# One encoder layer with grouped experts: entry order, first expert pair, and the order of the last factors

## The chip, the cores and the metric

The kernel runs on one core of a Trainium2 chip. The metric is the device time of one execution in microseconds. The kernel before took 590.38 us as the median of three runs (590.33 to 591.84).

## The reference

Input x is (1, 512, 1024) in float32. One layer is computed, cut here to its order:

```python
h = layer_norm(x, ln_emb_g, ln_emb_b)
proj = h @ w_in                     # 1024 x 1824: qa, ka, va, cq, ckv, kr
out_a = windowed_gqa_sink(...)      # 8 heads of 64, keys within 128 positions, a sink per head
out_b = mla_attention(...)          # 8 heads, low-rank q (768) and kv (256), all keys
h = layer_norm(2**0.25 * h + concat(rms_norm(out_a), rms_norm(out_b)) @ w_out, ...)
# experts: the best of 4 groups, in it the best 2 of 8; 32 experts of 1024 -> 256 -> 1024
for e in range(32):
    y += combine[:, e:e+1] * ((silu(h @ w_gate[e]) * (h @ w_up[e])) @ w_down[e])
h = layer_norm(2**0.25 * h + y, ln_ffn_g, ln_ffn_b)
```

## The kernel before, in words

The 512 tokens are four tiles of 128 rows (t = 0 to 3); 1024 features are eight blocks of 128. Most products of the first part are made of three: each operand is split into a rounded high half (a copy on ScalarE) and a low half (a subtraction, mostly on VectorE), `split` at line 208, and `mm3` at 213 to 215 multiplies high by high, high by low and low by high.

**Entry.** SP issues x, then gain and bias of the first norm spread over all partitions (line 144), the constants, and the first chunk of `w_in` in four quarters (line 161). `layer_norm` (line 199) makes z[t] of x with two VectorE operations per half (lines 203 and 204); TensorE turns z into eight blocks (line 257), and their halves are `hth` and `htl`. The weight halves of the first chunk are split with their low part on GpSimd (line 209). Products of tile 0 with the first chunk are ordered by what arrives (line 385); all others run through `mm3`. z itself stays in memory as the residual.

**Middle.** Three more chunks of `w_in`, the low-rank key and query products (units of 4 heads and a tile; `heads` turns them, line 468), attention B, attention A, and the output projections, which add into z. Here the order on the engines is a planner's: it simulates the program and issues what is ready first, by order of the text, with a few orders laid down by `issue_after`.

**From the last attention tile to the end** the order on all engines is the written one (`manual_schedule`). The last two tiles (a = 2, b = 3) are normed, routed (`route`: ten small VectorE steps that end in the tile's expert mask), counted (`count`: products with a triangle, `place`: the row's place in its expert) and selected (`select`: a 0/1 matrix of 64 places per expert). The rows of the first expert pair are gathered by products (`gather`, line 1131); later pairs are fetched by an indirect DMA on GpSimd from the normed rows in HBM (`fetch`, line 1056), into which `keep` (line 847) writes them from ScalarE's queue.

**Experts.** They run in 16 pairs, 64 rows of each expert. A pair p takes eight blocks of gate and up products for both experts (`gates`, line 1265; 512 columns), `gated` (line 1269 on), the down products (`down`, line 1285), the weighted add into the rows (line 1298) and an indirect DMA that writes them to HBM (`scatter`, line 1291). Between hid and its transpose and after it, `meanwhile` does other work. Weights are 3 MB for each expert, in a ring of six slots, so three pairs are in memory or on their way. Slots 0 and 1 hold the gate weights of blocks 0 to 3 as two tiles of 512 KB and those of blocks 4 to 7 as one of 1 MB (`gu_tiles`); the other slots have two of 1 MB. A load into a slot waits until the products that read the old tile are done, and SP issues loads in order. `load_next(p)` asks for pair p + 3.

In pair 0 two blocks of gates go first, then the place products of pairs 0 to 3 (line 1394), the row numbers (lines 1027 to 1035) and four fetches, and the weights of the routing (lines 927 to 935); the other six blocks follow.

**End.** The last pair's rows go by products with the transposed selection (`pz_part`, lines 1332 and 1334) onto the rows read back from HBM; `total`, `square`, `factor` (a power on GpSimd, line 183), `gain_first` (line 1548) and `scale_bias` (line 1553) norm them, and SP writes them out.

## Time and profile before

| | |
|---|---|
| median of three runs | 590.38 us (590.33 to 591.84) |
| the profiled execution | 591.72 us, its span 590.0 us |
| TensorE busy | 532.0 us (90%) |
| VectorE busy | 319.1 us (54%) |
| ScalarE busy | 221.9 us (38%) |
| GpSimd busy | 97.3 us (16%) |
| DMA moved | 141.76 MB, mean 240 GB/s |

The span is the time from the first to the last instruction; the rest of an execution lies around it. Busy shares are means over stages that have different limits, so the rows below are taken by stretch. PE is TensorE, PEld its weight loads, DVE VectorE, ACT ScalarE, POOL GpSimd, SP the engine that issues most DMAs; L1265 is line 1265 of the kernel before. The granted clock is a share of full speed. What stands in brackets behind an instruction is the idle time ahead of it on its engine and what ended it.

### The profile page before, as it was taken

The page shows a single profiled execution, that of the slowest core. Times are in us where ns is not written, and L with a number is a line of the kernel's source. Part 1 is how long each engine was busy: PE and PEld are TensorE (multiplying, and loading weights), DVE is VectorE, ACT ScalarE, POOL GpSimd, SP SyncE. Part 2 cuts the span into 40 slices and gives each one's busy share as a digit, 9 for nine tenths or more (in the row PEclk, how much of TensorE's full clock was granted, in tenths as well). Part 3 has the DMA queues.
Part 4 walks back from the last instruction along what each step waited for, and adds up shares of the span by engine and source line. Part 5 has one row for each costly group of instructions (what it writes and reads, how often), then busy time and mean ns, then how long its engine had stood idle before and what let it go on. Part 6 is the DMA issues. An engine that isn't in the chain of part 4 may idle for free. (4 is left out here: it accounts for less than half of the span.)

```text
span 590.0 us, 8025 instructions
## 1 busy us (share of the span) xinstructions
PE 532.0 (90%) x2772; PEld 334.5 (57%) x2773; DVE 319.1 (54%) x870; ACT 221.9 (38%) x481; POOL 97.3 (16%) x139
## 2 busy tenths in 40 slices
PE   2899999999898999999998899999997699879883
PEld 1688898799765777677777444343432233314241
DVE  5955473765687757947768734434434222102266
ACT  2356442454587738856731312211111111102123
POOL 2701121311100000213200201122111101100031
PEclk9999999999898999999999989999999989979988
DMA  8982400121210005991266899999999999999673
GB/s 288 294 275 72 142 3 1 58 82 41 84 46 27 1 1 207 292 355 50 65 261 248 293 389 398 420 417 414 414 415 395 422 418 386 415 420 417 256 284 142
DMA packets 46267, 141.76 MB, mean 240 GB/s; under 512 B 12379, under 2 KB 19419, under 8 KB 37008
## 3 DMA queue, kind: packets, MB, share of 16 engines
q1 hardware_dynamic: 40608, 131.06, 58.8%
q0 software_dynamic: 4464, 8.06, 3.7%
q10 hardware_dynamic: 1152, 2.10, 0.9%
q8 instruction: 23, 0.38, 0.3%
q14 instruction: 20, 0.16, 0.1%
HBM read 133.14 MB, written 16.25 MB: 253 GB/s over the span
## 5 line engine op out<-in xcount | busy, mean ns | idle before, releaser
L1265 PE MATMUL p_gu<-w_gu,xT 128*64 128x512 f32 x512 | 125.4, 614 | 15.2 <-DMA w_gu<-in_w_gu 14.3
L1265 PEld LDWEIGHTS p_gu<-w_gu,xT 128*64 128x64 f32 x512 | 39.0, 141 | 96.8 <-issue 72.1
L1269 ACT ACTIVATE hid<-p_gu 128x256 f32<-128x256 f32 x16 | 6.1, 383 | 176.6 <-PE p_gu L1265 164.7
L1270 DVE TENSOR_TENSOR hid<-hid,p_gu 128x256 f32<-128x256 f32 x16 | 6.7, 421 | 113.8 <-ACT hid L1269 113.7
L1285 PE MATMUL p_y<-w_dn,hidT 128*64 128x512 f32 x256 | 59.8, 610 | 1.0 <-issue 0.6
L1298 DVE SCALAR_TENSOR_TENSOR xg<-p_y,wsl,xg 128x512 f32<-128x512 f32 x30 | 22.5, 751 | 28.3 <-PE p_y L1285 27.6
L604 PE MATMUL ptr<-cst,pr 128*128 128x128 f32 x208 | 34.0, 283 | 1.9 <-ACT pr L562 1.4
L1285 PEld LDWEIGHTS p_y<-w_dn,hidT 128*64 128x64 f32 x256 | 17.5, 140 | 31.3 <-issue 29.2
L1056 POOL DMA_INDIRECT xg<-norm_rows,tok x16 | 16.5, 1029 | 102.5 <-PE p_y L1285 16.6
L1291 POOL DMA_INDIRECT moe_rows<-xg,idx x15 | 15.5, 1036 | 98.1 <-DVE xg L1298 72.6
L604 PEld LDWEIGHTS ptr<-cst,pr 128*128 128x128 f32 x208 | 25.3, 146 | 9.4 <-ACT pr L562 2.8
L577 ACT ACTIVATE pr<-pmm,bnm 128x512 f32<-128x512 f32 x32 | 22.0, 687 | 12.0 <-DVE bnm L574 10.7
L574 DVE TENSOR_REDUCE bnm<-pmm 128x1 f32<-128x512 f32 x32 | 21.9, 687 | 7.1 <-PE pmm L215 6.8
L215 PE MATMUL pmm<-wh,htl 128*128 128x512 f32 (+1 forms) x64 | 23.9, 374 | 0.0
L213 PE MATMUL pmm<-wh,hth 128*128 128x512 f32 (+1 forms) x64 | 23.8, 372 | 0.0
L214 PE MATMUL pmm<-wl,hth 128*128 128x512 f32 (+1 forms) x64 | 23.5, 368 | 0.0
L562 ACT ACTIVATE pr<-pr,rc 128x512 f32<-128x512 f32 (+2 forms) x32 | 20.6, 645 | 4.1 <-DVE rc L560 3.8
L590 DVE CUSTOM_DVE_ANT_0 sm<-pmm,mask,nsink 128x256 f32<-128x256 f32 (+1 forms) x32 | 17.4, 544 | 7.7 <-PE pmm L587 6.5
L215 PE MATMUL pwo<-wh,htl 128*128 128x512 f32 (+1 forms) x56 | 20.7, 370 | 0.0
L214 PE MATMUL pwo<-wl,hth 128*128 128x512 f32 (+1 forms) x56 | 20.5, 367 | 0.0
L213 PE MATMUL pwo<-wh,hth 128*128 128x512 f32 (+1 forms) x56 | 20.5, 367 | 0.0
L1254 ACT ACTIVATE xg<-xg,of 128x1024 f32<-128x1024 f32 x15 | 17.2, 1148 | 8.5 <-PE p_x L1250 7.8
(348 smaller groups left out, 1166.8 us busy)
## 6 DMA issues: line engine op xcount, KB each, us to landing
w_gu<-in_w_gu SPq DMA_DIRECT2D x52, 1024.0 KB, 16.3
w_dn<-in_w_dn SPq DMA_DIRECT2D x20, 1024.0 KB, 18.5
w_gu<-in_w_gu SPq DMA_DIRECT2D x24, 512.0 KB, 16.6
w_dn<-in_w_dn SPq DMA_DIRECT2D x24, 512.0 KB, 14.4
wf<-in_w_in SPq DMA_DIRECT2D x12, 512.0 KB, 6.5
moe_rows<-zr SPq DMA_DIRECT2D x8, 512.0 KB, 7.5
rows<-moe_rows SPq DMA_DIRECT2D x8, 512.0 KB, 8.3
wf<-in_w_q_b SPq DMA_DIRECT2D x12, 192.0 KB, 2.3
```

The costliest lines, as they stand in the source:

```text
L213: PE.matmul(ps, ah, bh, start=first, stop=False)
L214: PE.matmul(ps, ah, bl, start=False, stop=False)
L215: PE.matmul(ps, al, bh, start=False, stop=last)
L562: SC.mul(pr[:, :n], pr[:, :n], rc)
L574: V.tensor_reduce(nm, sp, AX.X, ALU.max, negate=True)
L577: exps_.append(SC.activation(pr[:, :S], sp, AF.Exp, bias=nm, accum_out=den).ins)
L590: V.tensor_tensor_reduce(sm[:, :nk], sp[:, :nk], mask[:, mo:mo + nk], 1.0, nsink[:, h:h + 1], ALU.add, ALU.min, nm)
L604: PE.transpose(pt[:, k * P:(k + 1) * P], pr[:, k * P:(k + 1) * P], ident)
L1254: SC.mul(pl["xg"], pl["xg"], pl["of"])
L1265: PE.matmul(pg[64 * i:64 * i + 64], xT[:, j, 64 * i:64 * i + 64], ws[i][0][j], start=(j == 0), stop=(j == 7))
L1285: r = PE.matmul(py[64 * i:64 * i + 64, :], hT[:, j, 64 * i:64 * i + 64], ws[i][1][n][:, j], start=(j == 0), stop=(j == 1))
L1298: V.scalar_tensor_tensor(y, py, pl["wsl"], y, ALU.mult, ALU.add)
```

## The change

**Entry.** Gain and bias come in as columns (`ge_T`, one number per feature and partition) and are applied after the transposes: ScalarE scales and shifts x by the row's statistics into z, TensorE turns it, and `gain_x` applies gain and bias to 128x128 blocks on VectorE or ScalarE. The order for tiles 0 and 1 on VectorE, ScalarE, TensorE and GpSimd is written out; the low weight halves are made on VectorE. z then lacks gain and bias; they are loaded later and put on in the query units, half a tile behind each unit's `heads`.

**Routing.** Tile a's second gain and bias stand earlier, `route(a)` is stopped after five steps and resumed later, counts and places move, tile a and b are gathered from the second half, `rows_of` stands ahead of the copies of xT, and the rest of the routing goes behind the first place products.

**First pair.** The gate blocks run in the order 4 to 7, 0 to 3; behind the first of them come the place products of pairs 0 and 1 alone, their rows and the fetches 1 and 0, then the routing's end, then the other seven blocks. The places of pairs 2 and 3 come behind hid. After both halves of the down products, `between` makes the place products with the weights for four pairs, then pair 1's columns, then the residual, and only then the weighted adds. In slots 0 and 1 the second half of the gate weights is now in two tiles of 512 KB and the first in one of 1 MB; pair 3 loads the second half first, for both experts in turns.

**End.** `factor` stands one or more steps earlier.

```diff
+        geT = cp.tile([P, 2, NK], F32, name="geT")
+        SC.dma_start(out=cst, in_=A["cst"][:, :C_KEEP])
+        SC.dma_start(out=geT, in_=A["ge_T"])
         load_x(0)
-        lg, lb = [lp.tile([P, D], F32, name=nm) for nm in ("lng", "lnb")]
-        for n in range(2):
-            for dst, nm in ((lg, "ln_emb_g"), (lb, "ln_emb_b")):
-                SY.dma_start(out=dst[:, 512 * n:512 * n + 512], in_=A[nm][512 * n:512 * n + 512].partition_broadcast(P))
-        SY.dma_start(out=cst, in_=A["cst"][:, :C_KEEP])
...
-                split(wf[:, :, :n], wh[:, :, :n], wl[:, :, :n], PO if nch[0] == 0 else V)
+                if nch[0]:
+                    split(wf[:, :, :n], wh[:, :, :n], wl[:, :, :n])
+                else:
+                    wfs.append(wf)
...
-            layer_norm(xs[t], z[t], lg, lb)
+        chunks.append(chunk_load([(768, 512)]))
+        for t in range(2, NT):
+            load_x(t)
...
+        def scaled_x(t, kk):
+
+            rs, nb = nrm[t]
+            sl = slice(512 * kk, 512 * kk + 512)
+            SC.activation(z[t][:, sl], xs[t][:, sl], AF.Identity, scale=rs, bias=nb)
+
+        def turn_x(t, kk):
+            pt = ptr()
+            for k in range(4):
+                PE.transpose(pt[:, k * P:(k + 1) * P], z[t][:, (4 * kk + k) * P:(4 * kk + k + 1) * P], ident)
+            tur[t, kk] = pt, lp.tile([P, 4, P], F32, name="hf", bufs=2)
...
+        def gain_x(t, kk, ks, eng):
+            pt, hf = tur[t, kk]
+            for k in ks:
+                g_, b_ = [geT[:, i, 4 * kk + k:4 * kk + k + 1] for i in range(2)]
+                if eng is SC:
+                    SC.activation(hf[:, k], pt[:, k * P:(k + 1) * P], AF.Identity, scale=g_, bias=b_)
+                else:
+                    V.tensor_scalar(hf[:, k], pt[:, k * P:(k + 1) * P], g_, b_, ALU.mult, ALU.add)
...
+        def high(t, kk):
+            SC.copy(hth[at(t, kk)], tur[t, kk][1])
+
+        def low(t, kk):
+            V.tensor_tensor(htl[at(t, kk)], tur[t, kk][1], f32v(hth[at(t, kk)]), ALU.subtract)
+
+        def w_high(q):
+            SC.copy(chunks[0][1][q][0], wfs[q])
+
+        def w_low(q):
+            V.tensor_tensor(chunks[0][1][q][1], wfs[q], f32v(chunks[0][1][q][0]), ALU.subtract)
...
+        with tc.manual_schedule(engines={V.engine, SC.engine, PE.engine, PO.engine}):
+            stats_half(0, 0)
+            stats_half(0, 1)
+            stats_end(0)
+            stats_shift(0)
...
+                scaled_x(0, kk)
+                turn_x(0, kk)
+            gain_x(0, 0, range(4), V)
+            w_high(0)
+            stats_half(1, 0)
+            gain_x(0, 1, (1,), SC)
+            high(0, 0)
+            first_mm(0, hth, 0, 0)
+            low(0, 0)
+            first_mm(0, htl, 0, 0)
+            gain_x(0, 1, (3,), SC)
+            gain_x(0, 1, (0, 2), V)
+            w_high(1)
+            first_mm(0, hth, 1, 0)
+            first_mm(0, htl, 1, 0)
+            stats_half(1, 1)
+            stats_end(1)
+            high(0, 1)
+            low(0, 1)
+            stats_shift(1)
+            w_high(2)
+            first_mm(0, hth, 2, 0)
+            first_mm(0, htl, 2, 0)
+            for kk in range(2):
+                scaled_x(1, kk)
+                turn_x(1, kk)
+            w_low(0)
+            w_high(3)
+            first_mm(0, hth, 3, 0)
+            first_mm(0, htl, 3, 0)
+            gain_x(1, 0, range(4), V)
+            high(1, 0)
+            gain_x(1, 1, (0, 2), V)
+            gain_x(1, 1, (1, 3), SC)
+            low(1, 0)
+            high(1, 1)
+            low(1, 1)
+            first_mm(0, hth, 0, 1)
+            for q in range(4):
+                first_mm(1, hth, q, 0)
+                first_mm(1, htl, q, 0)
+            for q in range(1, 4):
+                w_low(q)
+                first_mm(0, hth, q, 1)
+            for q in range(4):
+                first_mm(1, hth, q, 1)
+        for t in range(2, NT):
...
+                if kk:
+                    gain_x(t, kk, range(4), SC)
+                else:
+                    gain_x(t, kk, range(4), V)
+                high(t, kk)
+                low(t, kk)
...
-                heads(qt_, qth, qtl, c, t)
+                with tc.issue_after(heads(qt_, qth, qtl, c, t)):
+
+                    zt = z[t][:, 512 * c:512 * c + 512]
+                    V.tensor_tensor(zt, zt, lgb[0][:, c], ALU.mult)
+                    V.tensor_tensor(zt, zt, lgb[1][:, c], ALU.add)
...
-        def load_turns(e, slots):
-
-            ws = [[], []]
-            for h in range(2):
+        def gu_tiles(slot, i):
+            if i == 1 and slot < 2:
+                return [(f"gu{slot}1{q}", 4 + 2 * q, 2) for q in range(2)]
+            return [(f"gu{slot}{i}", 4 * i, 4)]
+
+        def load_gus(e, slot, eng=SY):
+            return load_gu(e, slot, 0, eng) + load_gu(e, slot, 1, eng)
+
+        def load_turns(e, slots, order):
+
+            ws = [{}, {}]
+            for h in order:
                 for ts in zip(*[gu_tiles(sl, h) for sl in slots]):
                     for i in range(2):
-                        ws[i] += load_blocks(e + i, slots[i], *ts[i])
...
         norm_bias(a, 0)
+        norm_gain(a, 1)
+        norm_bias(a, 1)
         logits(a, 0)
         logits(a, 1)
...
         wout_l(1, p1_)
-        steps(route(a))
-        place(1)
+        ra = route(a)
+        steps(ra, 5)
         turn(b, 0)
-        count(a)
         add_z(1, p1_)
...
         rsqrt(rs, mv[:, 1:2], 1.0, LN_EPS / ALPHA ** 2)
         negmean(b)
         turn(b, 1)
-        place(a)
+        steps(ra)
+        place(1)
         sel0_(1)
-        sel0_(a)
         logits(b, 0)
         logits(b, 1)
         offset(b)
         for i in (1, 0):
             scaled(b, i)
-        norm_gain(a, 1)
         biased(b)
-        norm_bias(a, 1)
         for i in range(2):
             keep(a, i)
         gather(0, range(2))
+        count(a)
         gather(1, range(2))
         steps(route(b))
+        place(a)
+        sel0_(a)
         count(b)
-        gather(a, [0])
         gain(b, 1, V)
+        gather(a, [1])
         place(b)
         sel0_(b)
-        gather(a, [1])
+        gather(a, [0])
+        shift(b, 1, V)
         gain(b, 0, V)
-        shift(b, 1, V)
         shift(b, 0, V)
         gather(b, [1, 0])
         for i in (1, 0):
             keep(b, i)
         xT0 = wk[0].tile([P, NK, P], F32, name="xT", bufs=3)
+        for t in (1, a, b):
+            rows_of(t)
         SC.copy(xT0[:, 4:8], gk[1])
         V.tensor_copy(xT0[:, 0:4], gk[0])
-        for t in (1, a, b):
-            exps(t)
-        silu = wk[0].tile([P, 1], F32, name="silu", bufs=1)
-        V.memset(silu, 0.0)
-
-        SC.activation(silu, silu, AF.Silu)
-        for t in (1, a, b):
-            rows_of(t)
-        sels[1] = [select_tile(2, t) for t in range(NT)]
...
-        def down(hT, ws, put):
+        def down(hT, ws, put, between=None):
+            pys = []
             for n in range(2):
                 py = ps.tile([P, 512], F32, name="p_y", tag="pwo", bufs=2)
                 for j in range(2):
                     for i in range(2):
                         r = PE.matmul(py[64 * i:64 * i + 64, :], hT[:, j, 64 * i:64 * i + 64],
                                       ws[i][1][n][:, j], start=(j == 0), stop=(j == 1))
-                put(slice(512 * n, 512 * n + 512), py)
+                pys.append(py)
+                if not between:
+                    put(slice(512 * n, 512 * n + 512), py)
+            if between:
+                between()
+                for n in range(2):
+                    put(slice(512 * n, 512 * n + 512), pys[n])
             return r.ins
...
-                gus = load_turns(e, (s0, s1)) if p + 3 == NP - 1 else [load_gus(e, s0), load_gus(e + 1, s1)]
-                ws[p + 3] = [(gu, None) for gu in gus]
+                if p == 0 or p + 3 == NP - 1:
+
+                    ws[p + 3] = [(gu, None) for gu in load_turns(e, (s0, s1), (0, 1) if p else (1, 0))]
+                else:
+                    ws[p + 3] = [(load_gus(e, s0), None), (load_gus(e + 1, s1), None)]
...
-        def run_pair(p, xT, meanwhile):
+        def run_pair(p, xT, meanwhile, between=None):
             pg = new_gates()
             if p == 0:
-                gates(pg, xT, ws[p], 0, 2)
-                pi = psd("places")
-                for t in range(NT):
-                    for u in range(4):
-                        PE.matmul(pi[:, 2 * u:2 * u + 2], (sel0[t], sels[1][t])[u // 2][:, P * (u % 2):P * (u % 2) + P],
-                                  cmb[t][:, 2 * u:2 * u + 2, 0], start=(t == 0 and u == 0), stop=(t == NT - 1 and u == 3))
-                for g in range(2):
-                    for u, pl in enumerate(places_rows(pi[:, 4 * g:4 * g + 4], 2, 2, 1)):
-                        plc[2 * g + u] = pl
-                        fetch(2 * g + u, pl)
-                for t in range(1, NT):
-                    weights(t)
-                gates(pg, xT, ws[p], 2, 8)
+
+                order = 4, 5, 6, 7, 0, 1, 2, 3
+                gates(pg, xT, ws[p], order, 0, 1)
+                first_rows(0, sel0)
+                routing_end()
+                gates(pg, xT, ws[p], order, 1)
             else:
-                gates(pg, xT, ws[p], 0, 8)
+                gates(pg, xT, ws[p])
             load_next(p)
-            r = leave_rows(gated(pg, meanwhile), ws[p], plc[p])
+            r = leave_rows(gated(pg, meanwhile), ws[p], plc[p], between)
             load_next_dn(p)
             return r
...
+        def first_rows(g, sel):
+
+            pi = psd("places")
+            for t in range(NT):
+                for u in range(2):
+                    PE.matmul(pi[:, 2 * u:2 * u + 2], sel[t][:, P * u:P * u + P], cmb[t][:, 4 * g + 2 * u:4 * g + 2 * u + 2, 0],
+                              start=(t == 0 and u == 0), stop=(t == NT - 1 and u == 1))
+            for u, pl in enumerate(places_rows(pi, 2, 2, 1)):
+                plc[2 * g + u] = pl
+            for q in ((1, 0), (2, 3))[g]:
+                fetch(q, plc[q])
+
+        def routing_end():
+
+            sels[1] = [select_tile(2, t) for t in range(NT)]
+            for t in (1, a, b):
+                exps(t)
+            silu = wk[0].tile([P, 1], F32, name="silu", bufs=1)
+            V.memset(silu, 0.0)
+
+            SC.activation(silu, silu, AF.Silu)
+            for t in range(1, NT):
+                weights(t)
...
                 if p == 0:
                     if i == 0:
-                        residual(0)
-                    else:
-                        pi = psd("places")
-                        places_mm(pi, sel0, [weights_of(u) for u in range(2)], range(NT))
-                        places_weights(pi, [plc[0], plc[1]], 6, 3, 1)
+                        first_rows(1, sels[1])
                     return
...
-            last = run_pair(p, xT, meanwhile)
-            if p == 0:
+            def between():
+                for u, sel in ((0, sel0), (2, sels[1])):
+                    pi = psd("places")
+                    places_mm(pi, sel, [weights_of(u + v) for v in range(2)], range(NT))
+                    places_weights(pi, [plc[u], plc[u + 1]], 6, 3, 1)
+
                 for i in range(2):
                     columns(plc[1], i, nx)
-                pi = psd("places")
-                places_mm(pi, sels[1], [weights_of(2 + u) for u in range(2)], range(NT))
-                places_weights(pi, [plc[2], plc[3]], 6, 3, 1)
+                residual(0)
+            last = run_pair(p, xT, meanwhile, None if p else between)
+            if p == 0:
                 group_sel(2)
             elif p == 1:
...
-        y2 = [ring(slots(p)[0], f"gu0{k}", [P, D], F32R, "y2") for k in range(2)]
+        y2 = [ring(slots(p)[0], f"gu1{k}", [P, D], F32R, "y2") for k in range(2)]
...
         gain_first(0)
         total(1)
         square(1)
+        factor(0)
         gain_first(1)
-        factor(0)
+        factor(1)
         scale_bias(0)
         total(2)
         square(2)
-        factor(1)
         scale_bias(1)
         gain_first(2)
+        factor(2)
         total(3)
         square(3)
         gain_first(3)
-        factor(2)
+        factor(3)
         scale_bias(2)
-        factor(3)
         scale_bias(3)
```

## Rows read from the trace of the kernel before

**Rows 1.** Busy time by stretch: length, five engines, granted clock, DMA share, GB/s

```profile
200.00:295.00 95.00, 93.96 (x549) 70.70 (x549) 66.17 (x207) 63.03 (x166) 16.89 (x44) 1.00 0.44 151
...
320.00:330.00 10.00, 8.77 (x69) 6.92 (x68) 8.04 (x34) 3.07 (x11) 0.00 (x0) 1.00 1.01 404
330.00:342.00 12.00, 10.02 (x52) 5.00 (x53) 7.56 (x43) 1.76 (x4) 4.25 (x4) 0.89 0.79 255
...
340.00:342.00 2.00, 2.00 (x7) 0.75 (x8) 0.48 (x3) 0.00 (x0) 0.00 (x0) 0.50 0.88 346
```

**Rows 2.** TensorE's waits, 330 to 570 us: total, times, longest

```profile
PE p_gu L1265 <- DMA w_gu<-in_w_gu: 14.3, 8, 4.1
```

**Rows 3.** The entry: groups by line (minimum, median, maximum ns) and instructions in time

```profile
L209 POOL TENSOR_TENSOR wl<-wf,wh x4: 2380/2652/2847, 12.1 to 20.6; 128x1024 fp32r<-128x1024 f32 x4
...
L204 DVE SCALAR_TENSOR_TENSOR z<-z,ln_rs,lnb x8: 735/742/2844, 7.7 to 29.7; 128x512 f32<-128x512 f32 x8
...
3.67 1.36 DVE L192 BATCH_NORM_STATS2 ln_st<-xt 128x6 f32<-128x512 f32 x2 [2.63 <-DMA xt<-in_x]
...
L323 DVE SCALAR_TENSOR_TENSOR rp<-pwo,rq,ctb x4: 337/344/352, 132.3 to 153.6; 128x128 f32<-128x128 f32 x4
...
L209 DVE TENSOR_TENSOR htl<-ptr,hth x4: 631/670/690, 11.1 to 25.8; 128x512 fp32r<-128x512 f32 x4
...
40.79 1.23 DVE L209 TENSOR_TENSOR wl<-wf,wh 128x1024 fp32r<-128x1024 f32 x1 [0.97 <-ACT wh L208]
...
31.22 0.39 PE L213 MATMUL pwo<-wh,hth 128*128 128x512 f32 x1
```

**Rows 4.** Query stage and first attention: stretches, one operation's price, GpSimd's additions

```profile
130.00:155.00 25.00, 23.26 (x140) 22.18 (x139) 13.56 (x36) 10.76 (x22) 4.70 (x9) 1.00 0.19 61
155.00:175.00 20.00, 19.42 (x109) 13.47 (x108) 16.74 (x39) 16.11 (x37) 0.45 (x1) 0.91 0.12 32
...
322.12 0.68 DVE L1144 TENSOR_TENSOR z<-z,lngb 128x512 f32<-128x512 f32 x1
...
L332 POOL TENSOR_TENSOR qtok<-rp,rp x8: 454/458/1205, 133.1 to 155.7; 128x128 f32<-128x128 f32 x8
```

**Rows 5.** The first expert pair in time: start, duration, engine, line

```profile
326.71 0.69 DVE L1230 COPY xT<-p_g 128x512 f32<-128x512 f32 x1 [1.54 <-PE p_g L1131]
...
327.46 1.94 PE L1265 MATMUL p_gu<-w_gu,xT 128*64 128x512 f32 x8 [0.78 <-DVE gn L914]
...
329.32 1.95 PE L1394 MATMUL psd<-cmb,sel 128*128 128x2 f32 x16
...
331.20 5.37 PE L1265 MATMUL p_gu<-w_gu,xT 128*64 128x512 f32 x24
...
338.07 0.42 DVE L1270 TENSOR_TENSOR hid<-hid,p_gu 128x256 f32<-128x256 f32 x1
...
339.98 5.02 PE L1285 MATMUL p_y<-w_dn,hidT 128*64 128x512 f32 x16
...
346.74 5.80 PE L1265 MATMUL p_gu<-w_gu,xT 128*64 128x512 f32 x26
...
356.38 3.65 PE L1285 MATMUL p_y<-w_dn,hidT 128*64 128x512 f32 x16
```

**Rows 6.** SP's load issues for the fourth pair, merged and alone

```profile
329.42 9.15 SPq L696 DMA_DIRECT2D w_gu<-in_w_gu  x6
...
333.16 0.33 SPq L696 DMA_DIRECT2D w_gu<-in_w_gu  x1
```

**Rows 7.** The last pair's gates and the last two outputs in time

```profile
555.49 3.65 PE L1265 MATMUL p_gu<-w_gu,xT 128*64 128x512 f32 x14 [1.30 <-DMA w_gu<-in_w_gu]
...
583.10 1.42 DVE L1553 SCALAR_TENSOR_TENSOR rows<-rows,st,gb 128x512 f32<-128x512 f32 x2 [0.66 <-POOL st L183]
...
585.25 1.42 DVE L1553 SCALAR_TENSOR_TENSOR rows<-rows,st,gb 128x512 f32<-128x512 f32 x2 [0.66 <-POOL st L183]
```

More of the change, by code (lines that the diff above doesn't have):

```diff
@@ L1298, in put @@
                 V.scalar_tensor_tensor(y, py, pl["wsl"], y, ALU.mult, ALU.add)
-            r = down(hT, ws, put)
+            r = down(hT, ws, put, between)
             scatter(pl)
@@ L1494, in build @@
                     pg = new_gates("pwo")
[L1495 removed]
+                    gates(pg, xT2, w_)
                     leave_rows(gated(pg), w_, pl)
```

121 lines of the change are left out of this document (68 added, 53 removed).

## The prediction, made before the result was known

> **What bounds the kernel now.** I read the stages first (busy time by stretch), then what TensorE waits for, then the queue that issues the loads, then the instructions around the first expert pair and at both ends. The reader is to see three regimes in [rows 1]. Up to about 310 us TensorE is the bound: 93.96 of 95 us busy between 200 and 295, and VectorE and ScalarE have room. From about 320 on the expert weights are: 404 GB/s in the ten microseconds from 320, and after the prefetched pairs are used up TensorE stands 14.3 us in eight waits for gate weights [rows 2]. Between these lies one hole: from 330 to 342 the transfers reach only 255 GB/s. After the last weights a tail of VectorE work ends the run. So an early saving counts as long as TensorE is dense, a saving in the hole counts because the stream never idles afterwards, and a saving in the tail counts in full. All sums are against the profiled execution, 591.72 us (span 590.0 and 1.72 around it). It lies near the top of the three runs, 1.34 above their median of 590.38, so I take the same difference off the median.
>
> **The entry.** Removed: the broadcast loads of gain and bias (four of 256 KB) ahead of the first weights, the two-step layer norm on VectorE, and the low halves of the first weight chunk on GpSimd. There each of four took 2.65 us, and the VectorE steps beside them stretched from 0.74 to 2.84 us [rows 3]. Added: ScalarE scaling of the rows, gain and bias on the transposed blocks (12 of 128x128 on ScalarE, 20 on VectorE), the weight lows on VectorE, and a written order for tiles 0 and 1. What matters is when tile 2's products can begin, since TensorE is dense behind them; before, tile 2's second product is at 31.22. VectorE's work up to there, after the change: six half statistics of 0.68 (4.1), 16 gains, priced by the 128x128 read from PSUM at 0.34 (at its pitch 0.3: 4.8), six low halves of 0.67 (4.0), four weight lows of 1.23 (4.9), three small chains of about 1 (3.0): 20.8 from 3.67 on gives 24.5. The first chain cannot be filled (factor on GpSimd, one scaling, eight transposes of a cold start): about 3 more, 27.5. Tile 2's transposes are behind both times, so the gain is near 31.0 - 27.5 = 3.5; I take **3.0**. From above: if tile 2's statistics slip into VectorE's gaps, 2.4 less work stands ahead, 5.4. From below: if ScalarE, which now carries scalings, casts and gains, sends VectorE waiting another 3 us, 0. The loads of the next chunk are issued earlier than now, as their buffers are freed earlier.
>
> **The residual gain and bias** come back as 16 VectorE operations of 128x512 on z, two behind each of the eight query units. Price 0.68 each, as the same operation on the same shape takes later [rows 4]: 10.9. Where they go VectorE has 25 - 13.56 = 11.4 us free while TensorE is busy 23.26 of 25 [rows 4], so most is covered by TensorE's products; the last two units' four operations (2.7) lie beside the first attention units, where VectorE is the busier engine (16.74 of 20). I take **+1.0**; ends 0 and 10.9. GpSimd's rope additions stand next to these operations: eight of 0.458 median, one of 1.205.
> The Trainium skill, page "SBUF — State Buffer", section "SBUF: two separate sides", says that VectorE operations with two SBUF inputs and GpSimd operations that read SBUF lock each other out of a shared port for a whole instruction. The trace bears this out at the entry (the 2.84 above). By that rule the removed GpSimd work is worth more, but here it speaks against the change: each new z operation may hold a rope addition, on which a query unit's transposes wait. The time that this would give is in the last rival.
>
> **Routing.** Moving tile a's second gain and bias forward fills VectorE time in which it waits for logits; stopping route(a) after five steps lets z of the last tile go first, about 1.3 us earlier, and the gathers close some 0.6 earlier. This does not move the restart of the weight stream, which hangs on the last projection product. The three row writes move into VectorE's wait of 1.54 ahead of its half of xT [rows 5]; without that cover they would cost 1.2. The gates begin with the half that ScalarE copies, so they need not wait for VectorE's 0.69: start about 326.4 instead of 327.46.
>
> **The ring's first release.** Now: of six gate loads for pair 3 the first is issued at 329.42, the second at 333.16, and the last is out 9.15 after the first began, since the second and third wait for later blocks and hold the other expert's loads behind them in SP's queue [rows 6]. After: one block (5.37 / 6 = 0.9), eight place products instead of 16 (half of 1.95), a second block: 329.2, and there **two** loads of 512 KB go, two more at 331.0, the two of 1 MB at 334.6. So 4.2 MB are asked for by 334.6 instead of 338.6. The hole is worth 12 x (404 - 255) / 404 = 4.4 us by bytes and 12 x 0.21 = 2.5 by DMA share [rows 1]. What is late next is pair 1's release. Pair 0 afterwards: select, exponents and weights keep VectorE until about 336, hid then instead of 338.07; the second rows (1.2 on VectorE, on the path between hid and its transpose) put the down products at 338.1 instead of 339.98; they take 3.65 as in pair 2 instead of 5.02; place products 2.0, columns 1.1, copy 0.6: gates of pair 1 at 345.5 instead of 346.74 [rows 5]. The stream is fed until about 349.6 and pair 1's first release comes near 349.0, so almost all of the gain holds: **3.3**, ends 1.0 and 4.4. The fetches change place: 1 before 0, and 2 and 3 behind hid; pair 2's columns need theirs only some 16 us later. The first pair's residual and scatter go about 2.5 later on ScalarE and GpSimd; the next user of that buffer is a fetch some 14 us behind.
>
> **The tail.** The last pair's final loads are now two blocks instead of four. TensorE waited 1.30 for the last one and then worked 3.65 [rows 7]; after, half of that follows: 1.8, taken as **1.6**, with 0 as the lower end if down weights or the rows read back arrive later. Putting factor(t) ahead of other VectorE work takes away the two waits of 0.66 for GpSimd's factor and the small step in front of each: **1.4** (0.7 to 1.4).
>
> **The sum:** -3.0 + 1.0 - 3.3 - 1.6 - 1.4 = -8.3. That is 583.4 for the profiled execution and 590.38 - 8.3 = **582.1** at the median.
>
> **Rivals.**
> A, the hole only moves: TensorE idles around the first hid as now (two idle stretches of about 1.2), its granted clock falls again to 0.50, the lower of the two levels, as in 340 to 342 [rows 1], the down products take 5.02, pair 1's release is late and the stream runs dry there. Ring term 1.0: 584.4. For it: the same idle did it before. Against: the idle stretches are shorter, with products between them.
> [...]
> B, the entry gives nothing and the z operations cost 3: 590.38 + 3 - 3.3 - 3.0 = 587.1. For it: four engines in a written order, each waiting for another. Against: 3.5 us of loads taken out of the way.
> C, it does not do what it says: the stream is not what ends, since the last pairs are paced by TensorE. Ring and last load nil: 590.38 - 3.0 + 1.0 - 1.4 = 587.0. Against: the 14.3 us of waits, of which the last is in the last pair. B and C together: 592.0.
> D, slower: the z operations lie on the path. All 16 uncovered and each of eight rope additions held as long as the longest (0.75) cost 10.9 + 6.0 = 16.9 against 9.3 of gains: 598.0. It decides from 55% of that price. For it: VectorE is 84% busy right behind, and the planner may spread the operations into attention. Against: 11.4 us free where they are issued.
>
> **How the numbers follow.** Forecast 0.60, A 0.13, B 0.06, C 0.04, B with C 0.05, D 0.12. A measurement here tells about 0.3%, 1.8 us, from no change. Faster: 0.60 + 0.13 + 0.06 + 0.04 = 0.83; same 0.05; slower 0.12. Low end: entry 5.4, ring 4.4, z 0, tail 3.2 give 577.4, rounded to 577.0; the high end takes in A, B and C: 588.5.
>
> **What would show it.** Tile 2's first product by 28; no stretch below 350 GB/s between 330 and 342; pair 1's gates near 345.5 minus the entry's gain; TensorE's last wait for gate weights followed by half as many products; no VectorE wait for the factor in the last two tiles. Wrong if attention starts no earlier than now, or if the hole reappears behind pair 1's gates.

## The result, and the profile after

Median before 593.58 us (590.33 to 595.50, 20 runs), after 590.32 (588.05 to 594.10, 20 runs): ratio 0.995, 95% interval 0.9934 to 0.9967. The change saves 3.0 us (2.0 to 3.9), where 8.3 were forecast. The forecast was also set off a median of three runs, 590.38; over twenty the kernel before stands 3.2 higher, so the absolute time missed by both. In what follows a ratio is turned into us with 593.3, and what stands in brackets behind a ratio or a saving is its 95% interval.

The runs of one kernel scatter over 4 to 8 us, and the mean granted clock of TensorE goes with it: over the 20 runs of the changed kernel -3.0 us per 0.01 of it (correlation -0.71). One profile therefore can't stand for a kernel; steps are compared below over the profiles of all kernels that share the code of the step. The profile of the changed kernel itself is of 592.95 us, and has a fall of the clock to 0.50 (309.7 to 316.6, in the routing) that ten of the thirteen profiles with this routing lack.

The stretches of the changed kernel that answer to [rows 1] (columns as there):

```profile
320.00:330.00 10.00, 9.77 (x83) 8.54 (x82) 9.01 (x34) 2.10 (x3) 0.12 (x1) 1.00 1.00 399
330.00:342.00 12.00, 10.01 (x52) 4.59 (x52) 8.44 (x50) 3.10 (x12) 3.40 (x4) 0.94 1.02 412
342.00:346.00 4.00, 4.00 (x16) 1.08 (x12) 0.00 (x0) 0.00 (x0) 0.85 (x1) 0.77 0.99 392
352.00:356.00 4.00, 4.00 (x22) 1.29 (x18) 2.19 (x6) 0.00 (x0) 1.10 (x1) 1.00 0.71 216
```

The hole of 330 to 342 is gone (255 GB/s then, 412 now), and a smaller one stands at 352 to 356 (216 GB/s, where the kernel before has 376), as rival A said. TensorE's waits over the whole run, against [rows 2]:

```profile
PE p_gu L1383 <- DMA w_gu<-in_w_gu: 11.3, 4, 4.3
PE pz L1457 <- DMA rows<-moe_rows: 2.6, 1, 2.6
```

Four of the eight waits for gate weights are gone, 3.0 us of 14.3, and a new one is there: for rows read back in the tail. The first pair, TensorE, VectorE and SP in time, against [rows 5, 6]:

```profile
329.02 1.08 PE L1383 MATMUL p_gu<-w_gu,xT 128*64 128x512 f32 x4
...
338.47 0.42 DVE L1388 TENSOR_TENSOR hid<-hid,p_gu 128x256 f32<-128x256 f32 x1
...
338.94 0.44 PE L1392 MATMUL p_t<-cst,hid 128*128 128x128 f32 x2 [0.72 <-DVE hid L1388]
...
340.17 0.43 DVE L1394 COPY hidT<-p_t 128x256 f32<-128x256 f32 x1
...
340.65 5.24 PE L1404 MATMUL p_y<-w_dn,hidT 128*64 128x512 f32 x16 [1.27 <-DVE hidT L1394]
...
349.38 0.65 PE L1383 MATMUL p_gu<-w_gu,xT 128*64 128x512 f32 x2 [0.24 <-ACT xT L1368]
...
332.11 5.95 SPq L817 DMA_DIRECT2D w_gu<-in_w_gu  x6
...
353.06 0.33 SPq L817 DMA_DIRECT2D w_gu<-in_w_gu  x1
```

The six issues take 5.95 instead of 9.15, as they should. But between the hidden product and the down products TensorE stands 0.72 and 1.27, the down products take 5.24 (3.65 forecast, 5.02 before), and pair 1's gates come at 349.38; SP's next release is at 353.06 (350.41 before), and the hole of 352 to 356 lies there.

### The profile page after: what moved, and what is told of

It is laid out like the page before. It is cut to its first block, busy times and chain, and to the rows that moved or that the text cites. A ratio compares the mean times of both kernels' runs of the same rounds, so it can differ in the third digit from the quotient of the medians.

```text
span 591.3 us, 8062 instructions
## 1 busy us (share of the span) xinstructions
PE 537.7 (91%) x2772; PEld 334.4 (57%) x2773; DVE 325.1 (55%) x898; ACT 232.8 (39%) x501; POOL 90.0 (15%) x135
## 4 chain that ended last, share of the span: by engine, by line
PE 50%; DMA 33%; DVE 10%; ACT 3%; issue 2%; SPq 1%; POOL 0%; DVEq 0%; POOLq 0%; ACTq 0%
DMA w_gu<-in_w_gu 28%; PE p_gu L1383 6%; PE pwo L211 5%; PE pwo L210 5%; PE pwo L209 5%; PE pmm L209 4%; PE pmm L210 4%; PE pmm L211 4%; PE ptr L725 3%; PE pac L1190 2%; PE pac L759 2%; PE p_y L1404 2%; PE pz L1457 1%; DMA rows<-moe_rows 1%; DMA xt<-in_x 1%
## 5 line engine op out<-in xcount | busy, mean ns | idle before, releaser
L695 DVE TENSOR_REDUCE bnm<-pmm 128x1 f32<-128x512 f32 x32 | 21.8, 683 | 7.5 <-PE pmm L211 7.2
L211 PE MATMUL pmm<-wh,htl 128*128 128x512 f32 (+1 forms) x56 | 20.8, 372 | 0.0
L210 PE MATMUL pmm<-wl,hth 128*128 128x512 f32 (+1 forms) x56 | 20.5, 367 | 0.0
L209 PE MATMUL pmm<-wh,hth 128*128 128x512 f32 (+1 forms) x56 | 20.4, 364 | 0.0
```

Of the source, the lines that this page charges most:

```text
L209: PE.matmul(ps, ah, bh, start=first, stop=False)
L210: PE.matmul(ps, ah, bl, start=False, stop=False)
L211: PE.matmul(ps, al, bh, start=False, stop=last)
L695: V.tensor_reduce(nm, sp, AX.X, ALU.max, negate=True)
```

## The experiments

Each is timed against the kernel before on the same chip, in 6 to 12 runs of its own. Where an experiment leaves work out, its text says which.

**e1, the entry and the z operations alone** (the diff's part up to the query units, on the kernel before).

> The kernel before with the new entry alone (transposed gain and bias, rows normalized on ScalarE, the written order of tiles 0 and 1, and the 16 VectorE operations that bring gain and bias back into z behind the query units); routing, first pair, ring and tail stay as before. If the prediction sized both terms rightly (entry -3.0, z operations +1.0) it is 2.0 us below the kernel before. If the trace of the changed kernel is to be believed (2.2 ahead at the first sum of squares, 1.0 ahead when the second attention begins, 1.4 ahead at its end), it is about 1.2 below. If the z operations eat the entry's gain whole, no difference. Mark to read: the start of the gathers, 318.2 in the kernel before and 320.7 in the changed one: about 317 here if the later start there comes from the routing's order, 320 if it comes from the entry.

Ratio 1.0011 (0.9987 to 1.0034): +0.7 us. The entry's gain is eaten whole.

**e2, everything but these.** The rest of the diff on the kernel before.

> The kernel before with everything of the change but the entry: routing, first pair, ring and tail are the changed ones, layer norm and z as before. By the prediction's terms (ring -3.3, last piece -1.6, factor -1.4) it is 6.3 us below the kernel before. By the other theory, that the hole between 330 and 342 only moves behind pair 1's gates and the last piece gives nothing because TensorE paces the last pair, only the factor's 1.4 and a ring term of up to 1.0 are left: 1.4 to 2.4 below. Mark: GB/s between 330 and 342 and between 346 and 358, and TensorE's granted clock between 338 and 346.

0.9982 (0.9957 to 1.0006): -1.1 us (-2.6 to +0.4), near the rival's figure and far from 6.3. Its 12 runs have a mean granted clock of 0.967, those of the kernel before 0.974. In its profile the down products take 6.51, and 342 to 352 is the new hole (279 and 203 GB/s).

**e3, the factor's order alone.**

```diff
         gain_first(0)
         total(1)
         square(1)
+        factor(0)
         gain_first(1)
-        factor(0)
+        factor(1)
...
```

> The kernel before with the changed order of the tail alone (each tile's factor ahead of the other VectorE work). Prediction's term: 1.4 us below the kernel before (0.7 to 1.4), VectorE's two waits of 0.66 for GpSimd's factor gone. Rival: the square on ScalarE or the output stores end the run and it is below by less than 0.3.

0.997 (0.994 to 1.0): -1.8 us, with an interval that holds the 1.4 and nearly nothing.

**e4, the changed kernel without the z operations.**

```diff
-                with tc.issue_after(heads(qt_, qth, qtl, c, t)):
-                    zt = z[t][:, 512 * c:512 * c + 512]
-                    V.tensor_tensor(zt, zt, lgb[0][:, c], ALU.mult)
-                    V.tensor_tensor(zt, zt, lgb[1][:, c], ALU.add)
+                heads(qt_, qth, qtl, c, t)
```

> The changed kernel without the 16 VectorE operations on z, so that the residual lacks the first norm's gain and bias (they are still applied on the transposed side); the broadcast loads stay. It prices the z operations: by the prediction's term 1.0 us below the changed kernel, that is about 4.3 below the kernel before. By the trace of the changed kernel (the lead falls from 2.3 at the query tokens to 1.0 at the second attention's first maximum) 1.3 to 2.8 below the changed kernel, 4.6 to 6.1 below the kernel before. If they are covered whole, the same as the changed kernel.

0.9874 (0.9844 to 0.9904): -7.5 us, 4.5 below the changed kernel (2.5 to 6.5). By this the 16 operations cost 4.5, not 1.0. Where, the stretches at the start of attention show (TensorE, weight load, VectorE, ScalarE, GpSimd, clock, DMA). The kernel before:

```profile
150.00:155.00 5.00, 3.29 (x21) 2.76 (x20) 2.65 (x7) 2.58 (x6) 1.65 (x4) 1.00 0.47 144
155.00:160.00 5.00, 4.83 (x21) 3.59 (x19) 3.77 (x10) 2.54 (x7) 0.45 (x1) 0.66 0.33 105
160.00:165.00 5.00, 4.97 (x28) 3.65 (x29) 4.37 (x13) 4.28 (x10) 0.00 (x0) 1.00 0.01 2
```

The changed kernel:

```profile
150.00:155.00 5.00, 2.35 (x13) 1.43 (x12) 4.21 (x9) 2.69 (x6) 2.09 (x4) 1.00 0.41 144
155.00:160.00 5.00, 4.45 (x18) 3.29 (x18) 5.00 (x13) 2.38 (x5) 0.80 (x1) 0.66 0.36 105
160.00:165.00 5.00, 3.75 (x20) 2.59 (x19) 5.00 (x13) 3.51 (x9) 0.00 (x0) 1.00 0.00 0
```

VectorE is full (5.00 of 5, twice) and TensorE does 10.54 of 15 instead of 13.09. Without the z operations it does 12.85, all of it at full clock:

```profile
150.00:155.00 5.00, 3.29 (x20) 2.47 (x19) 4.40 (x13) 3.32 (x8) 1.05 (x4) 1.00 0.45 147
155.00:160.00 5.00, 4.56 (x25) 2.96 (x22) 4.13 (x10) 3.91 (x10) 0.00 (x0) 1.00 0.27 102
160.00:165.00 5.00, 5.00 (x32) 3.12 (x30) 3.81 (x10) 4.55 (x12) 0.00 (x0) 1.00 0.00 0
```

GpSimd's rope additions in the changed kernel, against [rows 4]:

```profile
138.66 0.46 POOL L450 TENSOR_TENSOR qtok<-rp,rp 128x128 f32<-128x128 f32 x1 [6.20 <-DVE rp L449]
140.51 2.94 POOL L450 TENSOR_TENSOR qtok<-rp,rp 128x128 f32<-128x128 f32 x1 [1.38 <-DVE rp L449]
...
153.49 1.34 POOL L450 TENSOR_TENSOR qtok<-rp,rp 128x128 f32<-128x128 f32 x1 [2.73 <-ACT pr L698]
156.19 0.80 POOL L450 TENSOR_TENSOR qtok<-rp,rp 128x128 f32<-128x128 f32 x1 [1.36 <-ACT qth L583]
```

Three of the eight are held, 2.94, 1.34 and 0.80 against 0.46. The last ends at 156.99, 0.85 later than in the kernel before, though the first query copy on ScalarE was 2.32 earlier (129.47 against 131.79).

**f1, the z operations behind the key and value units; f2, only the first eight of them.**

f1, cut (its broadcast loads stand one pass of the loop earlier):

```diff
-                heads(kt_, kth, ktl, c, t)
+                with tc.issue_after(heads(kt_, kth, ktl, c, t)):
+
+                    zt = z[t][:, 512 * c:512 * c + 512]
+                    V.tensor_tensor(zt, zt, lgb[0][:, c], ALU.mult)
+                    V.tensor_tensor(zt, zt, lgb[1][:, c], ALU.add)
...
```

f2, which leaves out the z operations of the last four query units:

```diff
+                    if c:
+                        continue
                     zt = z[t][:, 512 * c:512 * c + 512]
```

> The changed kernel with its 16 VectorE operations on z kept, but put behind the eight key and value units instead of the eight query units (their two broadcast loads are issued one loop earlier). The kernel without these operations was 0.76 points of the time before below the changed one, 4.5 us, where the prediction had priced them at 1.0. If the price is one of place, because the last of them sit between the last query units and the first attention units, where VectorE then has no gap from 150.8 to 166.2 and TensorE stands, this kernel keeps nearly all of the 4.5: about 7 below the kernel before. If 10.9 us of VectorE work cost that wherever they stand, or GpSimd's copies beside the key units are held as its rope additions were, it is within 1 of the changed kernel, 2 to 4 below the kernel before.

> The changed kernel with the eight z operations of the first four query units alone; those of the last four, beside the start of attention, are left out (the second half of the residual lacks the first norm's gain and bias). If the price lies at that seam, 3 to 4.5 us below the changed kernel, 6 to 7.5 below the kernel before. If it lies in GpSimd's held rope additions, of which the longest (2.94 instead of 0.46) is among the first four units, 0 to 1.5 below the changed kernel, 3 to 4.5 below the kernel before.

f1: 0.9907 (0.9868 to 0.9946), -5.5 us; f2: 0.9915 (0.9883 to 0.9947), -5.0. Both lie between their theories. f1 wins 2.5 of the 4.5 by place alone, give or take 2.5; in its profile TensorE waits 1.7 for converted weights whose loads now stand behind the broadcasts. f2 leaves both halves with about the same price, each uncertain by 2; it doesn't tell the start of attention from the held additions.

**g2, the z operations one loop half earlier, loads left in place** (half 0 behind the last four key units, half 1 behind the first four query units).

```diff
+                if c:
+                    with tc.issue_after(r):
+                        back(t, 0)
...
+                if not c:
+                    with tc.issue_after(r):
+                        back(t, 1)
```

> The changed kernel with its 16 z operations moved one loop half earlier: half 0 behind the last four key and value units, half 1 behind the first four query units; the broadcast loads stay where the change has them, so that no weight load waits behind them (in the variant with all of them at the key units TensorE waited 1.66 for converted weights). If the seam to attention is what the operations cost, attention starts as in the kernel without them and the run is 3 to 4.5 below the changed kernel, 6 to 7.5 below the kernel before. If VectorE's 10.9 us cost it anywhere, 0 to 1 below the changed kernel.

0.9905 (0.9873 to 0.9937): -5.6 us, 2.6 below the changed kernel with the same work (0.5 to 4.8). VectorE is no longer full at the start of attention:

```profile
155.00:160.00 5.00, 4.56 (x23) 2.87 (x21) 4.13 (x11) 3.91 (x10) 0.00 (x0) 1.00 0.24 92
160.00:165.00 5.00, 5.00 (x32) 3.15 (x31) 3.65 (x9) 4.54 (x12) 0.00 (x0) 1.00 0.01 2
```

From 150 to 165 it does 12.31 of 15, and TensorE 12.85 as in e4. So some 2.6 of the price are the place. The 1.9 that still lie between g2 and e4 are not clear of nothing (-0.8 to 4.4). A mark that all profiles have speaks against them: the start of the last products with sums of squares, in the kernel before

```profile
305.90 1.05 PE L1166 MATMUL psd<-cst,asq 128*128 128x1 f32 x8 [0.29 <-ACT asq L1157]
```

With the old entry they start at 305.1 to 306.5 (the kernel before, e2, e3; mean 305.8). With the z operations where the change has them, 306.5 to 307.7 (the changed kernel, e1, f3, f4, g1, h1, h2; mean 306.9); one loop half earlier, 301.7 to 304.2 (g2, g4, h3; mean 302.6); without them, 301.0 and 305.5 (e4, g3; mean 303.3). f1 has 302.4, and f2 305.5 with 6.8 us at 0.50 on the way. By this mark their place in the change costs some 3 to 4, and one loop half earlier nothing is left that stands out of the spread, though GpSimd's addition of 2.9 is held in all three of these profiles. It also shows how far one profile can be trusted: e4 and g3 run the same code up to this mark and lie 4.5 apart. In g3 the clock is at 0.50 for 13.7 us on the way, in e4 never, and e4's profile is the fastest of its six runs. How much of e4's 4.5 is the clock is not shown.

**g3, the entry alone, no z operations, on the kernel before.**

> The kernel before with the new entry alone and without the 16 z operations (the residual lacks the first norm's gain and bias). It prices the entry by itself: 3.0 us below the kernel before by the prediction's term; 2.2 by the marks at the first sum of squares and the query tokens of the changed kernel. If part of what the kernel without z operations gained is that TensorE's clock does not fall at the start of attention, 4 to 5.

0.9963 (0.9933 to 0.9994): -2.2 us (4.0 to 0.4 saved). The entry is worth what the marks said.

**f3, the second places' rows behind the copy of the hidden columns.**

```diff
-                    if i == 0:
+                    if i == 1:
                         first_rows(1, sels[1])
```

> The changed kernel with the second places' rows taken behind the copy of the first pair's hidden columns instead of between the hidden product and its transposes. In the trace of the changed kernel VectorE works 1.3 us on them while TensorE stands 0.72 and 1.27, and the down products after it take 5.24 at a granted clock of 0.66, against 3.65 at full clock in the kernel without z operations. If the stand causes the lower clock and the late release of pair 1, the down products start about 1.0 earlier, take 3.65 and the run is 1.0 to 2.5 below the changed kernel. If the clock falls for other reasons, or the fetches of pairs 2 and 3 come later and hold the next columns, no difference to the changed kernel, within 0.8.

0.9956 (0.9931 to 0.9981): the changed kernel. The down products start 1.22 behind the hidden product instead of 1.76, and take 5.35 all the same: TensorE stands once for 1.71 instead of twice. The down products were expected 1.0 earlier and came 0.54 earlier: the place products that had filled time ahead of the first stand now come behind a longer one.

**g1 and h1, idle products in the stand.** An idle product is one whose result nothing reads.

```diff
+        def warm(xT, n):
+            pw = ps.tile([P, 512], F32, name="p_w", tag="pmm", bufs=2)
+            for k in range(n):
+                PE.matmul(pw[:64], xT[:, k, 0:64], xT[:, 4:8], start=True, stop=True)
...
+                    warm(xT, 5 if i else 3)
```

In h1 the product is `PE.matmul(pw[:64, :P], xT[:, k, 0:64], xT[:, 4], ...)`.

> The changed kernel with eight idle products (64x128 by 128x512 of the first columns, never read) where TensorE stands around the first pair's hidden columns: three behind the second rows' products, five between the transposes and the down products. No useful work is added or moved. If the stand makes the granted clock fall to 0.50 in the down products (3.65 at full clock, 5.24 to 6.51 in the changed kernel's variants whose clock fell there), they take 3.65, the stream needs about 51 us from the 40th to the 60th megabyte instead of 52.2 to 53.5, and the run is 1.0 to 2.5 below the changed kernel, 4.0 to 5.5 below the kernel before. If the clock falls whatever TensorE does there, no difference to the changed kernel.

> The idle products around the first hidden columns again, now of 128 columns instead of 512: the long ones took 0.86 each where 0.22 was meant, and so held the down products up by 4.3 while the clock did stay up. Three before and five behind the transposes now fill 0.65 and 1.1 of the stands of 0.72 and 1.27. If the stand is what brings the clock down, the down products take 3.65, the stream's 40th to 60th megabyte about 51 us (52.2 to 53.5 in the changed kernel and its variants whose clock fell), and the run is 0.5 to 2.0 below the changed kernel, 3.5 to 5 below the kernel before. If not, the clock falls there all the same and the run is that of the changed kernel.

g1: 1.0029 (1.0002 to 1.0057): +1.7 us; its products were four times too long, so it settles nothing. h1: 0.9952 (0.9923 to 0.9982), no different from the changed kernel, give or take 2.0. In its profile the products fill the stand and the down products run at full clock:

```profile
335.66 0.87 PE L1551 MATMUL p_w<-xT 128*64 128x128 f32 x6
336.48 0.44 PE L1392 MATMUL p_t<-cst,hid 128*128 128x128 f32 x2
336.85 1.31 PE L1551 MATMUL p_w<-xT 128*64 128x128 f32 x10
338.09 3.65 PE L1404 MATMUL p_y<-w_dn,hidT 128*64 128x512 f32 x16
```

But so they do in e4, f1, g2 and h2, which have the stand and no idle products there; in the changed kernel, e2, f2, f3 and f4 they don't. That the stand brings the clock down is not shown: with the times equal, the expected 0.5 to 2.0 was not seen.

What goes with the clock there can be read, though. I counted when the bytes moved from the start pass 40 and 60 million (the stream starts again at about 40). The kernel before, the changed one and h2, from the one mark to the other (last two columns: DMA share, GB/s):

```profile
317.62:371.89 54.27, 50.31 (x294) 27.23 (x294) 31.40 (x128) 12.22 (x24) 8.71 (x9) 0.97 0.96 369
```

```profile
321.47:373.68 52.21, 48.72 (x281) 25.48 (x281) 29.28 (x124) 12.02 (x24) 7.78 (x8) 0.97 0.98 383
```

```profile
319.55:370.03 50.48, 47.06 (x280) 25.08 (x281) 29.14 (x123) 12.00 (x24) 8.24 (x8) 1.00 1.00 396
```

With the old first pair it takes 53.4 to 55.9 (four profiles, mean 54.5); one of them, g3, has the down products at full clock too and takes 54.4. With the new one it takes 50.5 to 51.0 where the clock stays up all the way (e4, f1, g2, h1, h2: mean 50.7), 52.2 to 54.9 where it falls in the down products (the changed kernel, e2, f2, f3, f4: mean 53.2). h3, which has h1's idle products (below), lies between: its down products take 3.65, but the clock falls right behind them, from 342.4 to 345.8, while pair 1's columns and first gates run:

```profile
316.71:368.76 52.05, 50.70 (x297) 27.46 (x297) 29.20 (x123) 12.18 (x24) 7.64 (x7) 0.97 0.98 384
```

So the idle products did not hold the clock up through the whole of the first pair there. That the clock makes these 2 us is the plain reading of eleven profiles; no run sets the clock alone, so it is not shown.

**f4, the last pair's loads and gates in the old pieces.**

```diff
-  load_turns(e, (s0, s1), (0, 1) if p else (1, 0))
+  load_turns(e, (s0, s1), (1, 0))
...
-            gates(pg, xT, ws[p])
+            gates(pg, xT, ws[p], (4, 5, 6, 7, 0, 1, 2, 3))
```

> The changed kernel with the last pair's weights in the pieces and order of the kernel before: the final load of each expert is a block of four, and the last pair's products take them in that order. If the shorter last piece gives the predicted 1.6, this kernel is 1.6 above the changed one. If the end is set by the rows of pair 14 that are read back (in the changed kernel TensorE does its last pair without a wait and then stands 2.61 for these rows), it is the same within 0.5: TensorE waits 1 to 2 for the last gate weights again and as much less for the rows.

0.9967 (0.9945 to 0.9989) against 0.995: the difference, 1.0 (-0.6 to 2.6), fits 1.6 and nothing alike. The profiles say more: the last hidden product is 0.77 later than in f3, and the end 0.16: TensorE waits 0.6 for the rows instead of 2.8. The last piece's gain goes into that wait.

**h2, idle products in the tail's wait.**

```diff
+            for k in range(9 if (t, n) == (2, 0) else 0):
+                PE.matmul(pzs[t, n][:64, :P], ident[:, :64], ident, start=True, stop=True)
             for k, r in enumerate(rows):
```

> The changed kernel with nine idle products (64x128 by 128x128, overwritten before they are read) ahead of the first sums with rows read back in the tail, where TensorE stands 2.6 to 2.8 for these rows and the granted clock then is 0.50 for part of the next products. If the end now goes through TensorE's products of the last two tiles, as the chain of waits says, and the clock stays up, it is 1 to 2 below the changed kernel. If the clock falls for an earlier stand, or the end goes through VectorE, no difference within 0.5.

0.9914 (0.9885 to 0.9943): -5.1 us, 2.1 below the changed kernel (0.2 to 4.1). The chain that ended last, in f3, whose tail is the changed kernel's (start, duration, what):

```profile
551.67 7.61 DMA moe_rows<-xg,idx
...
561.37 8.05 DMA rows<-moe_rows
569.42 0.04 issue
569.46 3.44 PE pz L1457 x4
572.90 0.68 PE pz L1459 x2
573.59 1.72 PE pz L1457 x4
```

and in h2:

```profile
561.00 7.99 DMA rows<-moe_rows
568.99 0.04 issue
569.03 1.13 PE pz L1459 x2
570.15 0.47 PE pz L1461 x2
570.62 1.72 PE pz L1459 x4
```

Pair 14's scatter and the read of its rows (7.61 and 8.05) now set when the last tiles' sums begin, and the first of these then ran at half clock: 3.44 instead of 1.72. In h2 the clock is 1.00 from 565 to 575; in f3 it is 0.67 between 570 and 575. f3 first, then h2:

```profile
570.00:575.00 5.00, 5.00 (x11) 2.29 (x9) 4.96 (x12) 1.69 (x4) 2.46 (x3) 0.67 0.28 115
570.00:575.00 5.00, 5.00 (x16) 2.81 (x15) 4.96 (x14) 2.86 (x7) 2.06 (x2) 1.00 0.12 49
```

That the idle products keep the clock up is borne out by both: all eleven profiles of the new tail without them have a fall to 0.50 between 562 and 580; h2 and h3 have none before 579. From the 130th million of bytes to the end they take 46.1 and 46.4, the eleven 47.4 to 48.7.

**g4 and h3, the pieces together.** g4 is g2 with g1's long products, h3 is g2 with h1's short ones and h2's.

> The changed kernel with the z operations moved one loop half earlier and the eight idle products around the first hidden columns: the version that both readings point to. If both are right it is 4.5 to 6.5 below the changed kernel, 7.5 to 9.5 below the kernel before; if the idle products do nothing, as the one with the z operations moved alone.

> The changed kernel with the z operations one loop half earlier, the short idle products around the first hidden columns and those in the tail. If all three readings are right: 2.7 for the place of the z operations (measured), 0.5 to 2.0 and 1 to 2 more: 7.5 to 10 below the kernel before. If the idle products give nothing: 5.6 below, as with the z operations moved alone.

g4: 0.9949 (0.9918 to 0.998), -3.0 us, spoilt by the same long products: from the 40th to the 60th million of bytes it takes 56.9, g2 50.8. h3: 0.9861 (0.9815 to 0.9906), -8.2 us, median 585.20: below both kernels, and about what g2 (5.6) and h2 (2.1) make together.

## Why the prediction was wrong

The steps by their terms; "measured" is a ratio where a kernel isolates the term, else profiles.

- **The entry**, -3.0: measured -2.2 (g3). Tile 2's products stand at 30.45 (before 31.22), not by 28, yet the lead reached 2.3 at the first query copy. Right in kind, a little large.
- **The z operations**, +1.0: measured +4.5 (e4, 2.5 to 6.5), or +2.8 between e1 and g3 (0.6 to 5.1). This is the step that failed most. I counted VectorE's free time over the query stage, 11.4 of 25 us, and let 10.9 us of work lie in it. But only eight of the operations ran ahead of the first attention product (137.17 to 147.3; it comes at 149.89); the other eight, not the four that I counted, ran beside the first attention units, from 151.40 to 163.2. There VectorE is the bound: without a gap from 150.8 to 165.9, TensorE short of 2.6 us of work. I had named four of these operations (2.7 us, "VectorE is the busier engine") and still took the price of covered ones. Rival D had the mechanism; its total of 16.9 was far too high and its chance of 0.12 too low for a milder form. Its held additions are there too: 2.48, 0.88 and 0.34 beyond 0.46. GpSimd's longest one, 2.94, spans five VectorE operations with two SBUF inputs, issued without a gap between them; but g2 keeps this hold and is 2.6 faster all the same, so the place is the larger part. The Trainium skill, page "SBUF — State Buffer", section "SBUF: two separate sides", says that a VectorE operation with two SBUF inputs and a GpSimd operation that reads SBUF block each other for a whole instruction; the trace agrees in kind, though here the hold lasted over several instructions.
- **Routing**, nothing counted for the stream: it is so. From the sums of squares' products to the stream's first load it takes 7.9 before (305.90 to 313.83) and 7.9 in e2, f3 and f4. To the first columns' copy it is 19.9 before and 18.6 in ten profiles of the new order (21.8 in three where the clock fell in it); these 1.3 stand in the ring's figure.
- **The ring**, -3.3: measured by the bytes -3.8 where the clock stays up, -1.3 where it falls in the down products, some half of the profiles each. The queue's order did what it should; the forecast took 3.65 for the down products, and rival A's 5.0 or more came in five of the nine profiles without idle products there. 0.13 was too low a chance for it. Its argument was misread, though: the kernel before has not two idle stretches of about 1.2 around the first hid but one of 1.98, and the new order has not shorter ones but the same time in two, 0.72 and 1.27:

```profile
338.55 0.44 PE L1274 MATMUL p_t<-cst,hid 128*128 128x128 f32 x2 [1.98 <-DVE hid L1270]
```

Pair 1's gates also wait for two sets of place products (2.4 us, 2.0 in the forecast), of which one stood beside TensorE's wait before. At full clock they come 18.7 to 19.1 behind pair 0's in the new order (e4, f1, g2, h1, h2; 19.1 forecast), 17.4 in the old (g3): the gain is the earlier first release alone.

- **The last piece**, -1.6, and **the factor**, -1.4: from the 130th million of bytes to the end 48.4 in three profiles of the old tail, 47.9 in ten of the changed one: 0.5 for both. The factor's order alone (e3) has 47.5, and the new tail with the old pieces (f4) 48.0, so the last piece is the term that gave next to nothing. I had set its lower end at 0 "if down weights or the rows read back arrive later", and that is what came: TensorE does the last pair without a wait and then stands 2.61 for the rows that pair 14 wrote. And the two waits of 0.66 are gone [rows 7], but VectorE waits 1.45 for ScalarE's sum of the last tile instead:

```profile
583.45 0.21 DVE L1679 TENSOR_SCALAR st<-st 128x1 f32<-128x1 f32 x1 [1.45 <-ACT rows L1676]
...
585.15 2.73 DVE L1698 SCALAR_TENSOR_TENSOR rows<-rows,st,gb 128x512 f32<-128x512 f32 x4
```

Put together: entry and z operations +0.7 (e1, with both), ring -2.5 (the mean of its two cases), tail -0.5: -2.3, against a saving of 3.0 (2.0 to 3.9) measured. With g3's -2.2 and the 4.5 of e4 instead it would be -0.7, and e1 and e2 as timed make -0.4, give or take 2.0. So the parts are known to about 2 us each and no better. Of the 5.3 that were missed, 2.7 lie in entry and z operations (-2.0 forecast), 0.8 in the ring and 2.5 in the tail, 6.0 in all.

Left open: what makes the clock fall in the first pair of some executions and not of others, how much of the 4.5 in e4 is the clock, and whether the z operations one loop half earlier cost anything at all.

## What to carry to other kernels

Free time of an engine over a stage covers nothing by itself: work is covered only where it runs, so look at the ten microseconds around each place, above all at the seam to a stage where that engine becomes the bound. Taking the last wait off one engine's tail is worth only the distance to the next chain, so follow the second one too (here scatter, read back, sums) before a term is booked whole. A handful of idle products in a known wait on TensorE can be worth more than shortening what leads up to it (h2's 2.1 us against next to nothing from the last piece), but only where the products behind the wait are the path; in the first pair they gave nothing that could be measured.

## What the runs showed of the hardware

The same program on the same chip differs by 4 to 8 us from run to run, and with the mean granted clock: -1.4 to -4.1 us per 0.01 in the kernels timed here. A GpSimd addition of 0.46 took 2.94 beside five VectorE operations in a row. A scatter of 64 + 64 rows took 7.61 us while the DMA engines moved 194 GB/s. The read of the rows behind it, eight loads of 512 KB, took 8.05 from issue to landing, with the DMA engines busy throughout at 398 GB/s. Nine idle products of 128 columns in a wait of 2.6 to 2.8 us on TensorE went with a clock of 1.00 behind it in both profiles that have them; all eleven of the same tail without them have 0.50 near it.
